# A decoder trunk's up-projection from seven block products in place of eight

## The chip, the cores and the metric

The kernel runs on one core of a Trainium2 chip. The metric is the device time of one execution in microseconds, lower is better. The core's engines are named as the profile names them: PE (TensorE) multiplies matrices and PEld is its loading of weights, DVE, ACT and POOL work elementwise, SP issues transfers; each has its own instruction stream and waits for others by semaphores.

## The reference

One step of a hybrid decoder: a token mixer with two parallel head groups, then a convolutional feed-forward layer (ConvFFN). One prompt of 2048 rows with 16 meta rows ahead, and 8 samples of 4 rows, go through the same weights. Only the ConvFFN concerns this change:

```python
def conv_ffn(h, buf, w_up, cw, cb, w_down):
    u = h @ w_up                           # (rows, 1024) @ (1024, 6144)
    u, new_buf = causal_dwconv(u, buf, cw, cb)   # 3 taps along the rows
    g, v = u[..., :D_FF], u[..., D_FF:]    # 3072 gate and 3072 value columns
    return (jax.nn.gelu(g) * v) @ w_down, new_buf
```

All is float32.

## The kernel before

**Exactness.** A product of float32 operands is formed from two parts of each operand in a rounded format (`F32R`): `hi` is the operand rounded, `lo` is what is left. `group_mm` and `tile_mm` issue three matmuls for each pair of 128-wide blocks: hi by hi, hi by lo, lo by hi. For weights, `split_w` makes the parts `whi` (ACT, L104) and `wlo` (DVE, L105) each time that a block of 512 KB has been loaded; each of the four super-tiles loads and splits all weights anew. There are two raw slots (`wraw`) and two slots for each part.

**Phases.** `phase_a` runs the mixer in six super-tiles; it ends at 930.4 us of the span. `phase_b` runs the ConvFFN in four super-tiles of 512 prompt rows (`PLAN_B`); the first has 34 rows more (`"m"`: 32 sample rows and 2 meta rows). Phase A's last part writes the normalized, transposed and split rows of the first one (`Normed.turn`, tiles `hhi` and `hlo`).

**One super-tile.** `up_g` and `up_v` run over kk = 0 to 23. Each takes one 128-column group of the up-projection, contracts it in 8 chunks of 128, and so issues 24 matmuls of 512 rows (the first super-tile: 48, in pieces of 274 and 272 rows). ACT copies the product from PSUM to `u`; ACT (L842) and DVE (L844, twice) form the convolution; ACT the gelu (L850); DVE the product `p` and its parts `phi` and `plo`. After each 4 kk (`NB`), `down` multiplies that block's `p` by two loaded blocks of `w_down` for one half of the output columns: for each of four row tiles 12 matmuls of 512 columns, added to `acc` by DVE (L887). In the first super-tile `samples` (L910) also multiplies the raw, unsplit `w_down` block by the sample rows. The first half of a block's downs stands two kk after the block, and the second half after the next block.

**Order.** PE follows the order of the program list (`prog`). DVE, ACT and POOL follow an order that a scheduler made ahead of the run, from `START2` to near the end. Loads are issued on SP in the order in which the weights are used, two ahead (`AHEAD`). All engines are strictly in order.

The reader needs of the code: `load_w`, `split_w` and `group_mm` for the weights, `up`, `up_g`, `up_v` and `down` for the stage, and the loop at the end of `phase_b` for the order.

Of the kernel before, what the change touches and what calls it, by code (L numbers as in the profile page):

```python
# [7 lines left out]
F32 = mybir.dt.float32  # L8
# [8 lines left out]
P = 128  # L17
# [10 lines left out]
PLAN_B = [["m", 0, 1, 2, 3], [4, 5, 6, 7], [8, 9, 10, 11], [12, 13, 14, 15]]  # L28
# [3 lines left out]
NFMAX = 546  # L32
# [3 lines left out]
GT_BUFS = 2  # L36

# side tasks of a super-tile, by the main unit that they follow
# [33 lines left out]
def build(tc, i, o):  # L72
# [5 lines left out]
    with contextlib.ExitStack() as es:  # L78
# [6 lines left out]
        phase = es.enter_context(contextlib.ExitStack())  # L85

# [9 lines left out]
        def load_w(src):  # L96
            raw = wp.tile([P, 1024], F32, name="wraw", tag="wraw", bufs=2)
            ld(raw, src)
            return raw

        def split_w(raw, E=V):
            hi = wp.tile([P, 1024], F32R, name="whi", tag="whi")
            lo = wp.tile([P, 1024], F32R, name="wlo", tag="wlo")
            A.activation(hi, raw, AF.Copy)  # L104
            E.tensor_tensor(lo, raw, hi.bitcast(F32), op=SUB)  # L105
            return hi, lo, raw
# [20 lines left out]
        def rstd_tile():  # L127
            return hp.tile([P, 1], F32, name="rstd", tag="rstd", bufs=8)

        def sum_squares(x, rows, width):  # L130
            ss = hp.tile([P, 1], F32, name="nss", tag="nss", bufs=8)
            junk = hp.tile([P, D], BF16, name="junk", tag="junk", bufs=1)
            A.activation(junk[:rows, :width], x, AF.Square, accum_out=ss[:rows])
            return ss
# [7 lines left out]
        class Normed:  # L142
            """rows of x normalized, transposed and split, tile by tile"""
# [6 lines left out]
            def alloc(self):  # L150
                if self.h is None:
                    self.h = [hp.tile([P, 8, NFMAX], F32R, name=nm, tag=nm) for nm in ("hhi", "hlo")]

            def load(self, q):
                src, off, rows = self.tiles[q]
                x = self.x[q] = hp.tile([P, D], F32, name="x", tag="x", bufs=3)
# [27 lines left out]

        def add(fn, *srcs):
# [16 lines left out]
        h_b = Normed(b_tiles(k, 0, None))  # L202
# [3 lines left out]
        flat = [s for fn, srcs in prog for s in srcs]  # L206
        raws, split, used = [], [], 0
# [3 lines left out]
        for n, (fn, srcs) in enumerate(prog):  # L211
# [5 lines left out]
            ahead = AHEAD if n >= START2 else 0  # L217
            while len(raws) < min(len(flat), used + len(srcs) + AHEAD):
                raws.append(load_w(flat[len(raws)]))
            while len(split) < min(len(flat), used + len(srcs) + ahead):  # L220
                split.append(split_w(raws[len(split)], V if split else G))
            ws = split[used:used + len(srcs)]
# [7 lines left out]
def b_tiles(k, si, acc):  # L230
    tiles, off = [], 0
    for q, t in enumerate(PLAN_B[si]):
        rows = SROWS + 2 if t == "m" else P
        if acc is None:
            tiles.append((lambda t=t: (k.x2m if t == "m" else k.x2d[t], True), off, rows))
        else:
            tiles.append((lambda q=q: (acc[q][1], False), off, rows))
        off += rows
    return tiles
# [38 lines left out]
def phase_a(k, h_b):  # L278
# [27 lines left out]
    def setup():  # L306
        ca = k.phase.enter_context(k.tc.tile_pool(name="ca", bufs=1))
        sp = k.phase.enter_context(k.tc.tile_pool(name="sa", bufs=2))
        E.ca, E.sp = ca, sp
        packed = ca.tile([P, SMALL_W], F32, name="packed", tag="packed")  # L310
# [52 lines left out]
def phase_a_tile(k, E, c, si, columns, norm, norm2, x_src):  # L363
# [9 lines left out]
    def tmp(nm, width=NMAX + 3, bufs=2, rows=P, tag=None):  # L373
        return E.sp.tile([rows, width], F32, name=nm, tag=tag or nm, bufs=bufs)
# [25 lines left out]
    # step sizes  # L400
# [9 lines left out]
    def dt_turn():  # L410
        dt = T_.dt = E.sp.tile([P, 3, 8], F32, name="dt", tag="dt")
# [8 lines left out]
        T_.dtA = E.sp.tile([P, 3, 8], F32, name="dtA", tag="dtA")  # L420
        V.tensor_tensor(T_.dtA[:, :nt, :], dt[:, :nt, :], c["alog"][:, None, :].to_broadcast([P, nt, 8]), op=MUL)
        dh = E.sp.tile([P, 3, 8], F32R, name="dh", tag="dh")
        dl = E.sp.tile([P, 3, 8], F32, name="dl", tag="dl")
# [7 lines left out]
    def decays():  # L431
        """exp of the running, remaining and total sums"""
# [66 lines left out]
    def chunk2(q):  # L499
# [13 lines left out]
        Gm = E.sp.tile([P, 2, P], F32, name="Gm", tag="Gm", bufs=1)  # L513
# [46 lines left out]
    def chunk3(q):  # L560
# [3 lines left out]
        # two heads at a time, each on half of the array's columns  # L564
# [36 lines left out]
    # recurrent unit  # L601
# [109 lines left out]
    # output projection  # L711
# [375 lines left out]
```

## Time and profile before

| | us |
|---|---|
| three runs: lowest, median, highest | 2599.92, 2600.65, 2602.12 |
| span of the profiled execution | 2596.3 |
| PE busy | 2521.5 (97%) |
| DVE, ACT, POOL busy | 1770.5 (68%), 1191.7 (46%), 624.7 (24%) |
| traffic of the transfers | 294.56 MB, mean 113 GB/s |

The profiled execution has no device time of its own on the page beside its span; the span lies 4.4 us under the median of the runs, and that difference is taken for what lies around it. The page gives busy time per engine, groups of instructions with the mean duration of one, and the chain of work that ended last, followed back from the end. A group's row reads: line, engine, operation, output and inputs, shape, count, then busy us and mean ns of one, then the engine's idle time just ahead and what ended it. A row of the chain reads: start in us, duration in us, what ran, how often.

### The profile page before, as it was taken

To read this page: it belongs to the slowest core of one execution; us is meant where nothing else is said; L and a number is where in the kernel's file an instruction comes from. 1 tells how busy PE (TensorE), PEld (TensorE's weight loads), DVE (VectorE), ACT (ScalarE), POOL (GpSimd) and SP (SyncE) were. 2 spreads that over 40 slices of the span, in tenths; PEclk is the share of its full clock that TensorE was granted. 3 is DMA by queue.
4 is the path that set the end of the run, shared out by engine and by line. 5 is a ranking of instruction groups with operands and counts; after the bars stand their busy time and mean duration, and the time that the engine had idled before them with its cause. 6 is when DMAs were issued, how large, how long until landed. Compare 5 with 4: busy or idle time off the path is not lost.

```text
span 2596.3 us, 35012 instructions
## 1 busy us (share of the span) xinstructions
PE 2521.5 (97%) x13242; PEld 2152.7 (83%) x13242; DVE 1770.5 (68%) x2500; ACT 1191.7 (46%) x1861; POOL 624.7 (24%) x945
## 2 busy tenths in 40 slices
PE   7999999999999899999999999999999999999998
PEld 6788888888888799999987888888888888888887
DVE  7878889788888866555557655557655557655555
ACT  5445555455554654334435333335433334433333
POOL 5524333242333322112113111112111111111111
PEclk9999999999999999999999999999999999999999
DMA  5352341523415372222225222224222223222222
GB/s 186 120 178 90 102 168 71 180 90 127 152 66 191 111 237 83 98 82 82 82 82 180 88 92 98 97 98 139 100 94 98 92 95 122 97 91 90 96 98 96
DMA packets 89994, 294.56 MB, mean 113 GB/s; under 512 B 10760, under 2 KB 11144, under 8 KB 89824
## 3 DMA queue, kind: packets, MB, share of 16 engines
q1 hardware_dynamic: 89824, 292.32, 32.8%
q8 instruction: 104, 1.70, 0.3%
q14 instruction: 66, 0.54, 0.1%
HBM read 272.24 MB, written 20.03 MB: 113 GB/s over the span
## 4 chain that ended last, share of the span: by engine, by line
PE 81%; DVE 11%; ACT 3%; DMA 2%; issue 2%; POOL 1%; SPq 0%; DVEq 0%; POOLq 0%; ACTq 0%
PE mm L110 34%; PE yy L110 21%; PE sg L110 21%; DVE cv L397 3%; DVE wlo L105 2%; PE tr L178 1%; ACT whi L104 1%; DVE xi L642 1%; PE yy L567 1%; ACT cv L395 1%; PE sg L617 1%; DMA wraw<-in_w_in 1%; DVE xbc L493 0%; DMA x<-xo 0%; DVE L L520 0%
## 5 line engine op out<-in xcount | busy, mean ns | idle before, releaser
L105 DVE TENSOR_TENSOR wlo<-wraw,whi 128x1024 fp32r<-128x1024 f32 x455 | 565.1, 1243 | 539.8 <-ACT whi L104 538.9
L104 ACT ACTIVATE whi<-wraw 128x1024 fp32r<-128x1024 f32 x456 | 482.8, 1059 | 848.4 <-PE mm L110 425.6
L110 PE MATMUL mm<-hhi,whi 128*128 128x384 f32 (+5 forms) x1920 | 656.8, 342 | 12.8 <-ACT xr L392 9.4
L110 PE MATMUL mm<-hlo,whi 128*128 128x384 f32 (+5 forms) x1920 | 651.3, 339 | 0.9 <-DVE hlo L183 0.9
L110 PE MATMUL mm<-hhi,wlo 128*128 128x384 f32 (+5 forms) x1920 | 651.0, 339 | 0.0
L110 PEld LDWEIGHTS mm<-hhi,whi 128*128 128x128 f32 x1920 | 364.8, 190 | 44.5 <-ACT xr L392 11.2
L110 PEld LDWEIGHTS mm<-hlo,whi 128*128 128x128 f32 x1920 | 364.9, 190 | 28.8 <-DVE hlo L183 1.2
L110 PEld LDWEIGHTS mm<-hhi,wlo 128*128 128x128 f32 x1920 | 364.6, 190 | 24.4
L110 PE MATMUL yy<-hhi,wlo 128*128 128x512 f32 (+1 forms) x960 | 338.7, 353 | 0.0
L110 PE MATMUL yy<-hlo,whi 128*128 128x512 f32 (+1 forms) x960 | 337.7, 352 | 0.0
L110 PE MATMUL yy<-hhi,whi 128*128 128x512 f32 (+1 forms) x960 | 336.8, 351 | 0.0
L839 POOL COPY o_fc<-u 128x2 f32<-128x2 f32 x192 | 139.6, 727 | 767.7 <-ACT u L831 646.3
L844 DVE SCALAR_TENSOR_TENSOR c<-u,fcw,c 128x512 f32<-128x512 f32 (+1 forms) x384 | 293.4, 764 | 33.1 <-ACT c L842 23.4
L110 PE MATMUL sg<-whi,phi 128*128 128x512 f32 x768 | 306.7, 399 | 0.0
L110 PE MATMUL sg<-whi,plo 128*128 128x512 f32 x768 | 301.8, 393 | 0.0
L110 PE MATMUL sg<-wlo,phi 128*128 128x512 f32 x768 | 241.1, 395 | 0.0
L110 PEld LDWEIGHTS yy<-hlo,whi 128*128 128x128 f32 x960 | 180.8, 188 | 26.0
L110 PEld LDWEIGHTS yy<-hhi,whi 128*128 128x128 f32 x960 | 180.9, 188 | 25.4
L110 PEld LDWEIGHTS yy<-hhi,wlo 128*128 128x128 f32 x960 | 180.5, 188 | 24.5
L887 DVE TENSOR_TENSOR acc<-acc,sg 128x512 f32<-128x512 f32 x192 | 130.9, 682 | 76.9 <-PE sg L110 76.9
L110 PEld LDWEIGHTS sg<-whi,phi 128*128 128x128 f32 x768 | 144.5, 188 | 42.3 <-issue 8.4
L110 PEld LDWEIGHTS sg<-wlo,phi 128*128 128x128 f32 x768 | 144.4, 188 | 34.2
(223 smaller groups left out, 3226.3 us busy)
## 6 DMA issues: line engine op xcount, KB each, us to landing
wraw<-in_w_up SPq DMA_DIRECT2D x192, 512.0 KB, 3.5
wraw<-in_w_in SPq DMA_DIRECT2D x120, 512.0 KB, 3.5
wraw<-in_w_down SPq DMA_DIRECT2D x96, 512.0 KB, 3.5
wraw<-in_w_out SPq DMA_DIRECT2D x48, 512.0 KB, 3.5
x<-in_x_p SPq DMA_DIRECT2D x16, 512.0 KB, 5.4
xo<-in_x_p SPq DMA_DIRECT2D x32, 256.0 KB, 4.1
x<-xo SPq DMA_DIRECT2D x32, 256.0 KB, 4.0
acc<-x SPq DMA_DIRECT2D x16, 512.0 KB, 4.8
```

The lines of the kernel that those rows point to most:

```text
L104: A.activation(hi, raw, AF.Copy)
L105: E.tensor_tensor(lo, raw, hi.bitcast(F32), op=SUB)
L110: PE.matmul(ps, l, r, start=(k == 0), stop=(k == len(pairs) - 1))
L178: PE.transpose(ps[:, c * rows:(c + 1) * rows], x[:rows, (c0 + c) * P:(c0 + c + 1) * P], ident[:rows, :rows])
L395: A.activation(cv[:, 3:W], buf[:, 3:W], AF.Identity, scale=w[:, 3:4], bias=b)
L397: V.scalar_tensor_tensor(cv[:, 3:W], buf[:, t:t + NC], w[:, t:t + 1], cv[:, 3:W], op0=MUL, op1=ADD)
L567: PE.matmul(psy[z:z + 64, h // 2 * T:(h // 2 + 1) * T], Q.xdt[:T, h * 64:(h + 1) * 64], Q.L3[:, h, :], start=True, stop=True)
L617: PE.matmul(psa[:, :NC], c["wa"][:, j, :], xc[:, 3:W], start=True, stop=True)
L642: V.tensor_tensor_scan(h[:, 3:W], a4[:, j, 3:W], m4[:, j, 3:W], hc[:, j:j + 1], op0=MUL, op1=ADD)
L839: G.tensor_copy(o_fc[:, g, NS, :], u[:, W - 2:W])
L844: V.scalar_tensor_tensor(cv[:, 2:W], u[:, z:z + W - 2], fcw[:, g, z:z + 1], cv[:, 2:W], op0=MUL, op1=ADD)
L887: V.tensor_tensor(xv, xv, ps[:rows, :], op=ADD)
```

## The change

Each super-tile's rows are cut in two halves (256 rows; 274 in the first, with 16 sample rows and 2 meta rows each), the contraction in two halves of 512, and the columns in a gate block and a value block. The 2 by 2 by 2 block product of one kk then has 8 products of 12 matmuls; Strassen's algorithm (in Winograd's form) needs 7, with sums of the blocks as operands:

- On the rows' side, `Halves.turn` makes seven operand tiles `h0` to `h6` (plain blocks B11, B21, B22 and sums T1 to T4), each in two parts, once for a super-tile. They have one buffer each.
- On the weights' side there are the plain gate block (`whl`, two halves), the plain lower value block (`wv`) and four sums (`ws`, z = 0 to 3). In the first super-tile `Sums.split` makes them on POOL (L958 to L961) in place in the raw slots, splits each (ACT L106, DVE L107), and ACT's queue writes the parts to DRAM (`kept`, L964). The other three super-tiles load the parts from there (L951: 4 times 512 KB for each kk) and load of the value block only its lower half.
- The products' sums go through DVE: `s1` (ACT's copy), `s2`, `s3` and `put` (L1012), which adds the last product into `u`.

The code below is the core of the diff. It also lets go of several buffers to make room (phase A's pools, `acc` from 9 to 5 buffers, `xb` for the rows of the next super-tile with 2), forms a super-tile's rows from freshly loaded `x` (before: from `acc`), and loads `gfin` and `gffn` into one tile.

```diff
-PLAN_B = [["m", 0, 1, 2, 3], [4, 5, 6, 7], [8, 9, 10, 11], [12, 13, 14, 15]]
+PLAN_B = [[0, 1, 2, 3], [4, 5, 6, 7], [8, 9, 10, 11], [12, 13, 14, 15]]
+LOADS_B, SPLITS_B = 4, 3
...
+        class Halves:
+            def norm(self, q):
+                rows, load = self.tiles[q]
+                x = self.x[q] = k.hb.tile([P, D], F32, name="xb", tag="xb", bufs=2)
...
+    class Value:
+        def split(self, E=V):
+            hl = E_tile("wv", 512, 1)
+            k.divide(hl[:, 0], hl[:, 1], self.raw[:, 512:1024], E)
...
+    class Sums:
+        def load(self):
+            if not self.t.first:
+                self.out = E_tile("ws", 512, SUMS)
+                ld(self.out.bitcast(F32), kept[self.kk][self.z])
+        def split(self, E=V):
+            if not self.t.first:
+                return
+            g0, g1, v0, v1 = (x.raw[:, y:y + 512] for x in (self.g, self.v) for y in (0, 512))
+            if self.z == 0:
+                G.tensor_tensor(v1, v0, v1, op=ADD)
+                G.tensor_tensor(v0, g0, v0, op=SUB)
+                G.tensor_tensor(g0, v1, g0, op=SUB)
+                G.tensor_tensor(g1, g1, g0, op=SUB)
+            hl = self.out = E_tile("ws", 512, SUMS)
+            k.divide(hl[:, 0], hl[:, 1], (g0, v0, v1, g1)[self.z], E)
+            A.dma_start(kept[self.kk][self.z], hl.bitcast(F32))
...
+    def product(t, wts, z):
+        ps = psum(next(banks))
+        h = t.norm.h[z]
+        k.mms(ps[:, :t.N], [(wts[y1][:, n * P:(n + 1) * P], h[:, y2, n, 0:t.N])
+                            for n in range(4) for y1, y2 in ((0, 0), (0, 1), (1, 0))])
+        return ps
...
+    def second_part(t, kk):
+        def fn(v, w2, w3, w1, w4):
...
+            ps = product(t, (w2[:, 0], w2[:, 1]), T2)
+            q.s2, q.s3 = (tmp(nm, NHALF, 1)[:, :N] for nm in ("s2", "s3"))
+            V.tensor_tensor(q.s2, q.s1[:, :N], ps[:, :N], op=ADD)
+            ps = product(t, (w3[:, 0], w3[:, 1]), T3)
+            V.tensor_tensor(q.s3, q.s2, ps[:, :N], op=ADD)
+            ps = product(t, (w1[:, 0], w1[:, 1]), T1)
+            q.uv = tmp("u", UW, 3)
+            put(t, q.uv, 1, ps, q.s3)
+            V.tensor_tensor(q.s2, q.s2, ps[:, :N], op=ADD)
...
+    def third_part(t, kk):
+        def fn():
+            q = t.prev
+            put(t, q.uv, 0, product(t, (q.v[:, 0], q.v[:, 1]), T4), q.s3)
+            cv = conv(t, 24 + kk, q.uv)
+            put(t, q.ug, 1, product(t, (q.w4[:, 0], q.w4[:, 1]), B22), q.s2)
+            cg = conv(t, kk, q.ug)
...
+        for kk in range(24):
+            g = k.Plain(i["w_up"][kk])
+            v = Value(t, kk, g)
+            s2 = [Sums(t, kk, z, g, v) for z in range(4)]
+            add(first_part(t, kk), g)
+            if kk:
+                add(third_part(t, kk - 1))
...
+            add(second_part(t, kk), v, *s2)
```

One half of a block's downs now stands between the third and the second part at kk = 5, 6, 9, 10, 13, 14, 17, 18 and 21; the other three stand behind kk = 23.

The first place is PE in the first super-tile. Before, the rows of one group follow those of the group ahead of it; here is the end of a gate group's second piece and the start of the value group:

```order
L110 MATMUL mm_9438<-hhi_9121,whi_9325 128x272
L110 MATMUL mm_9438<-hlo_9122,whi_9325 128x272
L110 MATMUL mm_9438<-hhi_9121,wlo_9326 128x272
L110 MATMUL yy_9479<-hhi_9121,whi_9329 128x274
L110 MATMUL yy_9479<-hlo_9122,whi_9329 128x274
L110 MATMUL yy_9479<-hhi_9121,wlo_9330 128x274
```

Now, for kk = 7 (sums 10568 to 10713) with what stands around it; `h5`, `h6`, `h4` are T2, T3, T1, `h0`, `h1` are B11, B21, `h3` is T4 and `h2` is B22:

```order
L126 MATMUL yy_10623<-h0_8973,whl_10558 128x274 x12
L126 MATMUL mm_10638<-h1_8974,whl_10558 128x274 x12
L126 MATMUL tr_10654<-h3_8976,wv_10387 128x274 x12
L126 MATMUL yy_10676<-h2_8975,ws_10554 128x274 x12
L126 MATMUL mm_10731<-h5_8978,ws_10568 128x274 x12
L126 MATMUL tr_10747<-h6_8979,ws_10619 128x274 x12
L126 MATMUL yy_10761<-h4_8977,ws_10709 128x274 x12
L126 MATMUL mm_10782<-h0_8973,whl_10717 128x274 x12
```

Two groups of 48 matmuls have become seven of 12; the two products of kk = 6 that use `wv` and the last sum stand behind the first two of kk = 7.

The second place is POOL in the same stretch. Before it only copies the rows that the convolution carries over:

```order
L824 COPY u_10398<-st_fc_9386 128x8x2
L839 COPY o_fc_9392<-u_10115 128x2
L838 COPY o_fc_9392<-u_10183 128x16
L824 COPY u_10470<-st_fc_9386 128x8x2
L839 COPY o_fc_9392<-u_10183 128x2
L824 COPY u_10538<-st_fc_9386 128x8x2
```

Now the four sums of kk = 7 stand between such copies (`wraw2` is the raw value block, `wraw` the raw gate block):

```order
L1078 COPY o_fc_9388<-u_10615 128x2
L1075 COPY o_fc_9388<-u_10615 128x16
L958 TENSOR_TENSOR wraw2_10548<-wraw2_10548 128x512
L959 TENSOR_TENSOR wraw2_10548<-wraw_10546,wraw2_10548 128x512
L960 TENSOR_TENSOR wraw_10546<-wraw2_10548,wraw_10546 128x512
L1078 COPY o_fc_9388<-u_10418 128x2
L961 TENSOR_TENSOR wraw_10546<-wraw_10546 128x512
```

POOL's work on one kk has grown by four operations on 128 by 512 elements, in a row, each on what the one ahead wrote.

The third place is ACT there. Before, for one group and a half:

```order
L104 ACTIVATE whi_9896<-wraw_9894 128x1024
L836 ACTIVATE u_9832<-mm_9861 128x272
L842 ACTIVATE c_9889<-u_9832,fcb_9384,fcw_9382 128x560
L833 ACTIVATE u_9900<-yy_9902 128x8x4
L834 ACTIVATE u_9900<-yy_9902 128x242
```

Now, for kk = 7 (`wk7_0` is a sum's place in DRAM, L1057 the gelu):

```order
L1024 ACTIVATE s1_10636<-yy_10623 128x274
L106 ACTIVATE wv_10561<-wraw2_10548 128x512
L1080 ACTIVATE c_10672<-u_10615,fcb_9384,fcw_9382 128x560
L106 ACTIVATE ws_10568<-wraw_10546 128x512
L106 ACTIVATE ws_10619<-wraw2_10548 128x512
L1080 ACTIVATE c_10694<-u_10418,fcb_9384,fcw_9382 128x560
L964 DMA wk7_0_123<-ws_10568 128x1024
L964 DMA wk7_1_124<-ws_10619 128x1024
L1057 ACTIVATE c_10694<-c_10694 128x560
L106 ACTIVATE ws_10709<-wraw2_10548 128x512
L106 ACTIVATE ws_10713<-wraw_10546 128x512
```

Before, the splits stood among the copies out of PSUM; now one split of the value block and four splits of sums do, the last two of them behind the gelu, and ACT issues the writes.

The fourth place is SP's loads around a down call of the first super-tile. Before:

```order
L98 DMA wraw_10324<-in_w_up 128x1024
L98 DMA wraw_10392<-in_w_up 128x1024
L98 DMA wraw_10464<-in_w_down 128x1024
L98 DMA wraw_10532<-in_w_down 128x1024
L98 DMA wraw_10604<-in_w_up 128x1024
```

Now, around kk = 5 (L929 loads a value block):

```order
L929 DMA wraw2_10089<-in_w_up 128x1024
L117 DMA wraw_10083<-in_w_up 128x1024
L929 DMA wraw2_10321<-in_w_up 128x1024
L117 DMA wraw_10085<-in_w_down 128x1024
L117 DMA wraw_10087<-in_w_down 128x1024
L117 DMA wraw_10315<-in_w_up 128x1024
```

The value blocks have two slots of their own; gate blocks and `w_down` blocks still share two, and a gate block's slot is now also the place of two of the sums.

More of the change, by code (lines that the diff above doesn't have):

```diff
@@ L127, in rstd_tile, with sum_squares @@
         def rstd_tile():
[L128 to L133, printed above, removed]
+            return hp.tile([P, 1], F32, name="rstd", tag="rstd", bufs=4)
+        def sum_squares(x, rows, width, ss=None):
+            if ss is None:
+                ss = hp.tile([P, 1], F32, name="nss", tag="nss", bufs=4)
+            A.activation(junks[-1]()[:rows, :width], x, AF.Square, accum_out=ss[:rows])
             return ss
@@ L216, in build @@
                 begin.close()
[L217 to L222, printed above, removed]
+            b = n > k.begin_b
+            bound = len(flat) if b else next(z for z, w in enumerate(flat) if hasattr(w, "late"))
+            while loaded < min(bound, used + len(srcs) + (LOADS_B if b else AHEAD)):
+                flat[loaded].load()
+                loaded += 1
+            while split < min(bound, used + len(srcs) + (SPLITS_B if b else AHEAD if n >= START2 else 0)):
+                flat[split].split(*(() if split else (G,)))
+                split += 1
+            ws = [z.out for z in flat[used:used + len(srcs)]]
             used += len(srcs)
@@ L227, in build, with b_halves, samples, rows @@
             fn(*ws)
[L230 to L239, printed above, removed]
+def b_halves(k, si):
+    tiles, pairs = [], []
+    if si == 0:
+        def samples(x):
+            k.G.memset(x[:64], 0.0)
+            for r, a, n in ((0, 0, 16), (16, SROWS, 2), (32, 16, 16), (48, SROWS, 2)):
+                k.ld(x[r:r + n], k.x2m[a:a + n])
+            return x
+        tiles.append((50, samples))
+        pairs.append(((0, 0), (0, 32), MA, 0))
+    base, off = len(tiles), MA if si == 0 else 0
+    for z, q in enumerate((0, 2, 1, 3)):
+        def rows(x, q=q):
+            k.ld(x, k.x2d[PLAN_B[si][q]])
+            return x
+        tiles.append((P, rows))
+        if z % 2:
+            pairs.append(((base + z - 1, 0), (base + z, 0), P, off + z // 2 * P))
+    return k.Halves(tiles, pairs)
 def softplus_small(k, pool, x, n):
@@ L803, in phase_b @@
         t.si, t.first = si, si == 0
-        t.rows = [SROWS + 2 if z == "m" else P for z in PLAN_B[si]]
-        t.N = sum(t.rows)
-        t.W = F0 + 2 + (t.N - SROWS - 2) if t.first else t.N + 2
-        t.NP = t.N - SROWS - 2 if t.first else t.N
-        t.acc = []
-        t.norm = h_b if t.first else k.Normed(b_tiles(k, si, t.acc))
-        t.p, t.ss = {}, {}
+        t.N = NHALF if t.first else 256
+        t.u0 = F0 if t.first else 0
+        t.W = t.u0 + 2 + 512
+        t.acc, t.p, t.pm, t.ss = {}, {}, {}, {}
@@ new lines, in halves, with put @@
+    def halves(w, y):
+        return [w[z][:, y * 512:(y + 1) * 512] for z in range(2)]
+    B11, B21, B22, T4, T1, T2, T3 = range(7)
+    def put(t, u, half, ps, s):
+        N = t.N
+        parts = [(u[:, 2 + 256 * half:258 + 256 * half], 0, 256)]
+        if t.first:
+            u6 = u[:, 0:F0].rearrange("p (b k) -> p b k", k=6)[:, 4 * half:4 * half + 4, 2:6]
+            a = F0 + (2 + 256 if half else 0)
+            parts = [(u[:, a:F0 + 258 + 256 * half], 18 if half else 16, N), (u6, 0, 16)]
+        for out, a, b in parts:
+            src, oth = ps[:, a:b], s[:, a:b]
+            if b == 16:
+                src, oth = s4(src), s4(oth)
+            V.tensor_tensor(out, oth, src, op=ADD)
@@ L913, in samples @@
             if half == 0:
-                t.sacc = tmp("sacc", D, 1)
+                t.sacc = tmp("acc", D, 5)
             V.tensor_copy(t.sacc[:, hs], ps)
```

383 lines of the change are left out of this document (237 added, 146 removed), and 6 rows, old and new, of the table SLOTS.

## The prediction

> **What bounds the kernel now.** I read the stages first, then the chain that ended last within a stage, then the groups for the price of one instruction. The stages are phase A and the four super-tiles of phase B; the columns are length, then busy time of PE, PEld, DVE, ACT and POOL, granted clock, DMA share, GB/s:
>
> ```profile
> 0.00:930.40 930.40, 863.14 (x4971) 764.70 (x4972) 773.19 (x1238) 511.48 (x880) 348.61 (x438) 0.99 0.39 133
> 930.40:1378.80 448.40, 448.25 (x3025) 407.69 (x3025) 262.92 (x347) 186.05 (x323) 85.91 (x167) 1.00 0.30 103
> 1378.80:1783.70 404.90, 404.90 (x1761) 327.73 (x1761) 247.79 (x309) 167.87 (x226) 66.87 (x117) 1.00 0.31 106
> 1783.70:2188.05 404.35, 404.35 (x1762) 328.05 (x1761) 246.85 (x308) 167.38 (x225) 63.20 (x117) 1.00 0.30 103
> 2188.05:2596.30 408.25, 400.88 (x1729) 324.55 (x1727) 239.74 (x300) 158.96 (x209) 60.08 (x108) 0.99 0.28 98
> ```
>
> In phase B PE never waits: it is busy for 448.25 of 448.40 us, 404.90 of 404.90. So fewer matmul columns are worth their full time there, as long as PE still doesn't wait; and any wait that the change brings into phase B is paid in full, since there is no idle time of PE to hide it in. The chain of waits shows what one unit of work costs PE (start, duration, what, how often), first super-tile first, a full-width one last:
>
> ```profile
> 939.24 6.09 PE yy L110 x48
> 945.33 6.07 PE mm L110 x48
> ...
> 1116.10 1.00 PE sg L910 x8
> 1117.10 11.39 PE sg L110 x48
> ...
> 1378.80 5.58 PE mm L110 x24
> ...
> 1445.55 11.20 PE sg L110 x48
> ```
>
> A matmul of 272 or 274 rows takes 6.08/48 = 0.127 us, one of 512 takes 5.58/24 = 0.2325. A kk in the first super-tile (gate and value group) costs 12.15 us, and one with half a block's downs behind it 12.15 + 12.4 = 24.6.
>
> **The gain on PE.** Two groups per kk become seven products of 12. At the pace of before the first super-tile would fall by 24 × 12 × 0.127 = 36.6 us. For the others I need the pace of 256 rows, which phase A's last tile shows:
>
> ```profile
> 863.17 2.82 PE mm L110 x24
> ```
>
> That is 0.1175 us; I take 0.120, because every 12 matmuls now change both operand tiles. A super-tile of 256-row products is 24 × 84 × 0.120 = 241.9 us, its 576 down matmuls 576 × 0.2325 = 133.9. The turn of the next tile's rows is eight groups of four transposes, 0.44 us each by the row below, 4 us.
>
> ```profile
> 1372.77 0.44 PE tr L178 x4
> ```
>
> Ahead of the turn stand, for each row tile, a load and the norm (groups, and the last row from the table of loads, us from issue to landing):
>
> ```profile
> L133 ACT ACTIVATE junk<-x 128x1024 bf16<-128x1024 f32 x20 | 21.1, 1054 | 13.0 <-DMA x<-in_x_p 6.6 <-DMA x<-x 6.3
> L138 POOL TENSOR_SCALAR rstd<-nss 128x1 f32<-128x1 f32 x32 | 13.6, 425 | 172.7 <-ACT junk L133 169.4 <-ACT u L833 2.1 <-ACT xr L387 0.7
> L139 POOL TENSOR_TENSOR rstd<-rstd,neghalf 128x1 f32<-128x1 f32 x32 | 21.9, 685 | 2.5
> L168 DVE SCALAR_TENSOR_TENSOR x<-x,rstd,gain 128x1024 f32<-128x1024 f32 x20 | 25.7, 1284 | 16.1 <-POOL rstd L139 15.9
> ...
> acc<-x SPq DMA_DIRECT2D x16, 512.0 KB, 4.8
> ```
>
> Here is a new wait: `xb` has two buffers, so the third and fourth row tile are loaded only after the first two have been turned: load 4.8, sum of squares 1.05, `rstd` 0.43 + 0.69, scaling 1.28, together 8.3, with one row tile's downs of 12 × 0.2325 = 2.8 over it: about 6 us of idle PE per transition, 0 if the scheduler finds other cover, 8 without any. Super-tiles 2 and 3 then come to 241.9 + 133.9 + 4 + 6 = 386; the last has no turn but the 7.4 us of idle time that it has now (408.25 − 400.88), 383. Together −18.9 − 18.4 − 25.2 = −62.5. The same wait at the end of phase A, where the rows of the first super-tile pass through `xb`, I put at +8 (0 to 10).
>
> The other work of these three tiles is covered by PE: no weight of the up-projection but the plain gate and half a value block is split any more, and DVE's sum operations are new. Per kk DVE has two gate-and-value convolutions, product parts, splits and seven short sums, by the rows of the next fence at most 4 × 0.80 + 0.69 + 0.69 + 1.24 + 0.69 + 7 × 0.41 = 9.4 us under PE's 10.1. Tight, but the sums' loads lie ahead by four.
>
> **The loss: a loop in the first super-tile.** There the sums are made, and the waits go round in a circle with PE on it. `wv` has one buffer. So: T4 of kk−1 reads `wv` → ACT may write the next `wv` → DVE its second part → POOL L958 may overwrite that raw half → L959 → L960 → ACT and DVE split z = 0 → T2 of kk. PE has between T4 and T2 only B22, 12 matmuls or 1.5 us. The prices:
>
> ```profile
> L522 POOL TENSOR_TENSOR xdd<-xdt,ex 128x512 f32<-128x512 f32 x16 | 21.5, 1342 | 33.9 <-DVE xdt L517 33.9
> L585 POOL TENSOR_TENSOR S<-S,ex 128x512 f32<-128x512 f32 x16 | 19.7, 1229 | 25.4 <-PE yy L579 19.9 <-ACT gq L660 3.1 <-DVE xi L623 2.4
> L661 POOL TENSOR_TENSOR sacc<-sacc,gq 128x384 f32<-128x384 f32 x24 | 30.2, 1259 | 70.1 <-ACT gq L660 70.1
> L105 DVE TENSOR_TENSOR wlo<-wraw,whi 128x1024 fp32r<-128x1024 f32 x455 | 565.1, 1243 | 539.8 <-ACT whi L104 538.9
> L104 ACT ACTIVATE whi<-wraw 128x1024 fp32r<-128x1024 f32 x456 | 482.8, 1059 | 848.4 <-PE mm L110 425.6 <-PE sg L110 272.1 <-PE yy L110 69.7
> L183 DVE TENSOR_TENSOR hlo<-tr,hhi 128x512 fp32r<-128x512 f32 x64 | 43.4, 685 | 7.1 <-ACT hhi L182 6.9
> L182 ACT ACTIVATE hhi<-tr 128x512 fp32r<-128x512 f32 x64 | 37.6, 595 | 66.1 <-PE tr L178 66.0
> L514 DVE TENSOR_TENSOR Gm<-tr,packed 128x256 f32<-128x256 f32 x16 | 6.6, 413 | 0.5 <-PE tr L512 0.5
> L844 DVE SCALAR_TENSOR_TENSOR c<-u,fcw,c 128x560 f32<-128x560 f32 x96 | 76.9, 801 | 4.6 <-DMA sel<-in_sel 2.8
> L850 ACT ACTIVATE c<-c 128x560 f32<-128x560 f32 x24 | 16.2, 673 | 15.2 <-DVE c L844 15.0
> L870 DVE TENSOR_TENSOR p<-c 128x512 f32<-128x512 f32 x72 | 49.8, 692 | 2.5
> L867 DVE TENSOR_TENSOR pm<-c 128x32 f32<-128x32 f32 x24 | 4.6, 192 | 0.8
> ```
>
> Three POOL operations of 512 are 3 × 1.29 = 3.9 us (mean of the first two rows; the third row, 1.26 us for 384 elements, would make it 5.0). The first chain, from T4's end: `put` on DVE 0.6 (413 ns and a small one); in two of three cases a whole weight block's second part stands ahead on DVE, 1.24, so 0.8; `wv` second part 0.69; POOL 3.9; split 0.60 + 0.69: 7.3 us. A second chain starts at T2's end: `s2` 0.41, the last convolution step 0.80, gelu 0.67, behind which ACT's order puts the split of z = 2, then on DVE `pm` 0.19, `p` 0.69, second part 0.69: 3.4 us until T1 can run on, with T3 over part of it. On the loop stand T2, T1, B11, B21 and T4, 60 matmuls less 4 that need only a first part, 56 × 0.127 = 7.1. One kk: 7.1 + 7.3 + 3.4 = 17.8, against 12.15 now.
>
> That leaves PE idle for some 6 us once and 2 us once in each kk, and the clock answers to that. Windows at the end of phase A (PE alone: busy, clock, DMA share, GB/s):
>
> ```profile
> 846.00:850.00 4.00, 4.00 (x24) 0.68 0.36 131
> 851.00:854.50 3.50, 0.48 (x5) 0.97 0.41 150
> 854.50:858.00 3.50, 3.46 (x17) 0.55 0.42 150
> 858.00:862.00 4.00, 4.00 (x36) 1.00 0.00 0
> ```
>
> After 3 us with little on PE the clock was 0.55 for the next 3.5 us, then full. Half a clock for 3.5 us is at most 1.7 us of lost work; not each stall meets it, and part of it falls into the next wait, so +0.9 per kk: 18.7 (16 with POOL at 1.0 and no clock loss, 21 with POOL at 1.7). [...]
>
> In a kk with downs the loop is longer. The second `w_down` block takes the raw slot of the first, so it is loaded only behind the sample matmuls on that one, and ACT's order splits it behind all four sums of that kk, so behind POOL's fourth operation. The load (B22 1.5, samples 0.5, landing 4.8 by the row of `acc`) is the shorter way; the other gives from T4's end 0.6 + 1.24 + 0.69 + 4 × 1.29 + ACT 0.60 + 1.06 + DVE 1.24 and the handing over (0.2 to 0.3 us at each of seven semaphores) = 12.1 us, until the first row tile's third chunk can run. Then 41 of the 48 down matmuls are left, 41 × 0.2325 = 9.5, and the up products T2, T3, T1, B11, B21, T4, 72 × 0.127 = 9.1: 30.7, with 1.2 for clock 32 (27.5 if the second block is early, 35 with slow POOL), against 24.6.
>
> First super-tile: start 5, 15 × 18.7 = 280.5, 9 × 32 = 288, the rest (three down calls 33.5, last products, turn, samples, idle time between them) 59: 632, against 448.4: +184. Its bounds by the same terms: 15 × 16 + 9 × 27.5 + 55 = 542 (+94) and 15 × 21 + 9 × 35 + 70 = 700 (+252).
>
> The writes of the sums (50 MB, ACT's queue) and DVE's and ACT's added work in this tile cost nothing more: DVE has about 13 us in 18.7. If the loop were shorter, DVE would be late next.
>
> **Sum.** 2596.3 + 8 + 184 − 62.5 = 2725.8 us of span; the median lies 4.4 over the profiled span, so 2730.
>
> **Rivals.**
>
> *The loop is hidden and the kernel gets faster.* For it speaks that PE's work itself falls (by 36.6 in the first super-tile, 62.5 behind it) and that POOL is idle for 80% of this stage, so its operations could be shorter than phase A's busy ones. If POOL's operations took half (0.65), no block stood ahead on DVE and the second chain lay under T3, a kk would cost 7.1 + 4.6 + 1 = 12.5 and a kk with downs 25: first super-tile 187 + 225 + 59 = 471, and the end 2596.3 + 8 + 23 − 62.5 + 4.4 = 2569. It decides where a kk of the first super-tile loses less than (62.5 − 8)/24 = 2.3 us on the mean, that is at 14.4 us without downs; the wait from T4 to T2 would have to be under 4 us. Against it: no row shows POOL under 1.2 us for 512 elements. 7%.
>
> *The downs stay covered.* The second `w_down` block is split in time, so that only the kk without downs lose: 26 instead of 32, −54: 2676. 15%.
>
> *The transfers bound super-tiles 2 to 4.* A kk there loads 2.88 MB (four sums, one gate block, half a value block), against 1.05 now.
>
> ```profile
> 1378.80:1384.30 5.50, 5.50 (x25) 4.43 (x25) 4.50 (x7) 4.70 (x9) 3.00 (x5) 1.00 0.91 247
> 1384.30:1400.90 16.60, 16.60 (x73) 13.44 (x72) 14.93 (x17) 8.65 (x12) 7.42 (x10) 1.00 0.77 272
> ```
>
> At full share these give 247/0.91 = 271 and 272/0.77 = 353 GB/s, so 10.6 or 8.2 us for 2.88 MB against PE's 10.1. At 271, with the down blocks' loads between, 15 kk of three tiles lose 0.5 to 1.6 us: +24 to +72, 2754 to 2802. Against it: a whole tile moves 84 MB in 386 us, 218 GB/s. 18%.
>
> **Chances.** The forecast (both loops, transfers hidden) 57%, around 2730 with 2690 to 2775; downs covered 15%, transfers 18%, faster 7%, and 3% for an end within 0.2% (5 us, which is about what the measurement can tell). The range reaches from 2640, under the second case, to 2810 over the third. Slower 0.90, same 0.03, faster 0.07.
>
> **What would show it.** In the first super-tile PE busy some 70%, with T2's matmuls waiting for DVE's second part of z = 0 and that for L960; POOL L958 to L961 at 1.2 to 1.4 us; the granted clock under 1.0 there alone. Super-tiles 2 to 4 near 386, 386 and 383 us with PE over 97% busy, and idle PE of about 6 us at each transition, ended by transposes that wait for `xb`. The prediction is wrong if T4 to T2 takes under 4 us in the first tile, or if PE waits for loads of `ws` in the later ones.

## The result, and the profile after

The changed kernel takes 2871.26 us (median; 2869.09 to 2875.07) against 2601.1 for the kernel before beside it: a ratio of 1.1043, 95% interval 1.1027 to 1.1058. The forecast was slower, at 2730 with a range from 2640 to 2810: the direction was right, but the time lies over the range, and the loss of 270 us is twice the 130 of the forecast.

I cut both spans at the last transpose of each turn, which both kernels have. Before, the pieces are 930.1, 442.8, 407.8, 404.3 and 411.3 us. After (length, busy time of PE, PEld, DVE, ACT, POOL, granted clock, DMA share, GB/s):

```profile
0.00:974.70 974.70, 880.34 (x4977) 779.28 (x4978) 777.65 (x1249) 512.56 (x892) 326.82 (x447) 0.96 0.41 128
974.70:1674.10 699.40, 492.54 (x2679) 415.73 (x2677) 398.77 (x677) 209.89 (x321) 206.03 (x257) 0.83 0.38 138
1674.10:2077.30 403.20, 387.14 (x2651) 355.28 (x2649) 285.72 (x467) 161.10 (x238) 44.41 (x126) 0.99 0.64 227
2077.30:2472.90 395.60, 381.20 (x2626) 352.69 (x2625) 280.71 (x461) 159.42 (x232) 45.11 (x122) 0.99 0.64 226
2472.90:2867.20 394.30, 383.23 (x2631) 353.91 (x2629) 274.72 (x456) 150.49 (x219) 40.35 (x118) 0.99 0.60 213
```

So phase A lost 44.6 us, the first super-tile 256.6, and the other three gained 4.6, 8.7 and 17.0: +270.9, the difference of the spans. In the first super-tile PE is busy 70% of the time at a clock of 0.83. The chain of waits over one kk without downs there shows the loop (start, duration, what, how often):

```profile
1287.24 2.65 PE tr L126 x10
...
1293.65 1.54 PE mm L126 x10
...
1303.70 1.76 POOL wraw L958
...
1305.53 1.65 POOL wraw L959
...
1307.25 1.27 POOL wraw L960
...
1308.54 0.64 ACT ws L106
...
1309.20 1.22 DVE ws L107
...
1310.47 2.65 PE yy L126 x10
```

From T2 of one kk to T2 of the next are 23.2 us. Each of T2 and T1 shows ten of its twelve matmuls; the first two need only a first part and run ahead. T2's ten take 2.65 us, T1's ten 1.54. Windows over T2 and over T1 of one kk show the granted clock (third number from the end):

```profile
1287.24:1289.60 2.36, 2.36 (x10) 2.36 (x11) 1.26 (x2) 0.00 (x0) 0.61 (x2) 0.50 0.67 269
1293.65:1295.20 1.55, 1.55 (x12) 1.55 (x13) 1.15 (x2) 0.01 (x1) 0.00 (x0) 1.00 0.49 114
```

In this kk, behind the long wait (5.4 us up to T2's first two matmuls) the granted clock was 0.50; behind the short one of 1.3 us ahead of T1 it was 1.00.

What the forecast did not have lies ahead of L958; here are lines of PE, ACT, POOL and SP from the timeline of that stretch (start, duration, then in brackets the idle time before and what ended it):

```profile
1294.22 0.33 SPq L117 DMA_DIRECT2D wraw<-in_w_up  x1
1298.07 1.70 PE L126 MATMUL mm<-h,wv 128*128 128x274 f32 x12
1300.70 1.06 ACT L106 ACTIVATE whl<-wraw 128x1024 fp32r<-128x1024 f32 x1 [3.56 <-DMA wraw<-in_w_up]
1301.66 0.61 ACT L106 ACTIVATE wv<-wraw 128x512 fp32r<-128x512 f32 x1
1303.70 1.75 POOL L958 TENSOR_TENSOR wraw<-wraw 128x512 f32<-128x512 f32 x1 [3.12 <-DVE wv L107]
```

T4, which frees `wv`, is over at 1299.8; but ACT's order has the split of the next gate block ahead of the split of `wv`, and that waits until 1300.70 for its load. The load was issued only at 1294.22, when DVE had made the last second part out of that raw slot (z = 2 and 3 stand behind the gelu, and were done at 1294.20), and it took 6.5 us. L958 starts 3.9 us after T4, where the forecast's terms ahead of it come to 2.1 (0.6 + 0.8 + 0.69). In the 14 kk without downs counted below this distance is 3.6 to 5.4 us, 4.1 on the mean. Over the stage, the groups of the loop's operations read:

```profile
L959 POOL TENSOR_TENSOR wraw<-wraw,wraw 128x512 f32<-128x512 f32 x24 | 40.1, 1670 | 1.4
L958 POOL TENSOR_TENSOR wraw<-wraw 128x512 f32<-128x512 f32 x24 | 34.3, 1427 | 84.3 <-DVE u L1012 48.9 <-DVE wv L107 35.5
L960 POOL TENSOR_TENSOR wraw<-wraw,wraw 128x512 f32<-128x512 f32 x24 | 33.8, 1407 | 1.4
L961 POOL TENSOR_TENSOR wraw<-wraw 128x512 f32<-128x512 f32 x24 | 30.6, 1273 | 0.5
L107 DVE TENSOR_TENSOR ws<-wraw,ws 128x512 fp32r<-128x512 f32 x96 | 74.5, 814 | 58.1 <-ACT ws L106 58.1
```

L958 to L960 together cost 4.5 us, the forecast had 3.9. At the turn between super-tiles 2 and 3 (waits of PE: total, times, longest), and in the table of loads:

```profile
PE tr L225 <- DVE xb L215: 13.6, 2, 9.0
...
wk<-ws ACTq DMA_DIRECT2D x96, 512.0 KB, 4.7
...
wraw<-in_w_up SPq DMA_DIRECT2D x120, 512.0 KB, 4.9
```

Two waits for the next rows, 13.6 us, stand where the forecast had 6. A 512 KB block of `w_up` now takes 4.9 us from issue to landing at the median (before: 3.5).

For the first super-tile I give below the mean distance of two successive L960 in kk without downs (14 of them) and with downs (9). Here they are 24.3 and 31.7 us, against 18.7 and 32 in the forecast.

### The profile page after: what moved, and what is told of

The parts are those of the page before. It is cut to its first block, busy times and chain, and to the rows that moved or that the text cites. A ratio compares the mean times of both kernels' runs of the same rounds, so it can differ in the third digit from the quotient of the medians.

```text
span 2867.2 us, 42030 instructions
## 1 busy us (share of the span) xinstructions
PE 2524.5 (88%) x15554; PEld 2256.9 (79%) x15554; DVE 2017.6 (70%) x3306; ACT 1193.5 (42%) x1899; POOL 662.7 (23%) x1069
## 4 chain that ended last, share of the span: by engine, by line
PE 64%; DVE 15%; issue 7%; POOL 5%; ACT 4%; DMA 4%; SPq 0%; POOLq 0%; DVEq 0%; ACTq 0%
PE mm L126 23%; PE sg L126 16%; PE tr L126 10%; PE yy L126 10%; DVE whl L107 3%; DVE cv L496 3%; DMA wraw<-in_w_down 2%; POOL wraw L959 1%; ACT whl L106 1%; POOL wraw L960 1%; DVE ws L107 1%; POOL wraw L958 1%; ACT ws L106 1%; DMA xb<-x 1%; DVE c L1082 1%
## 5 line engine op out<-in xcount | busy, mean ns | idle before, releaser
L126 PE MATMUL sg<-whl,ph 128*128 128x512 f32 x2304 | 585.6, 412 | 27.5 <-ACT whl L106 11.7
L107 DVE TENSOR_TENSOR whl<-wraw,whl 128x1024 fp32r<-128x1024 f32 x359 | 452.7, 1262 | 206.1 <-ACT whl L106 205.9
L126 PEld LDWEIGHTS sg<-whl,ph 128*128 128x128 f32 x2304 | 446.9, 197 | 157.3 <-ACT whl L106 16.4
L106 ACT ACTIVATE whl<-wraw 128x1024 fp32r<-128x1024 f32 x360 | 380.1, 1057 | 390.8 <-PE sg L126 105.2
L126 PE MATMUL mm<-hhi,whl 128*128 128x384 f32 (+2 forms) x1920 | 487.8, 334 | 7.3 <-ACT xr L491 4.7
L126 PEld LDWEIGHTS mm<-hhi,whl 128*128 128x128 f32 x1920 | 348.3, 195 | 13.4 <-ACT xr L491 6.3
L1082 DVE SCALAR_TENSOR_TENSOR c<-u,fcw,c 128x512 f32<-128x512 f32 (+1 forms) x384 | 307.1, 828 | 43.1 <-ACT c L1080 41.2
L126 PE MATMUL mm<-hlo,whl 128*128 128x384 f32 (+2 forms) x960 | 316.1, 329 | 0.9 <-DVE hlo L199 0.9
L126 PE MATMUL mm<-h,ws 128*128 128x256 f32 (+1 forms) x1536 | 222.9, 296 | 47.9 <-ACT ws L106 41.3
L126 PE MATMUL yy<-h,ws 128*128 128x256 f32 (+1 forms) x1584 | 226.7, 293 | 41.5 <-ACT ws L106 31.8
L126 PE MATMUL tr<-h,ws 128*128 128x256 f32 (+1 forms) x1488 | 214.6, 295 | 43.5 <-ACT ws L106 37.7
L1057 ACT ACTIVATE c<-c 128x512 f32<-128x512 f32 (+1 forms) x96 | 61.6, 642 | 218.4 <-DVE c L1082 198.8
```

Of the source, the lines that this page charges most:

```text
L126: PE.matmul(ps, l, r, start=(k == 0), stop=(k == len(pairs) - 1))
L1057: A.activation(cg[:, 2:W], cg[:, 2:W], AF.Gelu_apprx_tanh)
L1082: V.scalar_tensor_tensor(cv[:, 2:W], u[:, z:z + W - 2], fcw[:, g, z:z + 1], cv[:, 2:W], op0=MUL, op1=ADD)
```

## The experiments

Each of the first ten is one run with a profile, beside one run of the kernel before on the same chip (2599.97 to 2603.45 us). "First super-tile" is always the stretch between last transposes, 699.4 us in the changed kernel.

**Shorter sums.**

```diff
-                G.tensor_tensor(v1, v0, v1, op=ADD)
+                G.tensor_tensor(v1[:, :8], v0[:, :8], v1[:, :8], op=ADD)
...
```

> The four POOL operations that make the sums run on 8 columns in place of 512 (so the sums are wrong), with the same reads, writes and waits between them; everything else is left. The scheduler, told of shorter operations, also puts the splits of z = 2 and 3 ahead of the gelu on ACT. Theory L (a loop from T4 over wv, POOL and z = 0 to T2 sets the pace of the first super-tile, and POOL's three operations of 1.27 to 1.75 us are over 4 us of it): a kk without downs falls from 24.3 to 16 to 19 us, one with downs from 31.7 to 25 to 28; the first super-tile from 696 to 530 to 590 us, the time to 2700 to 2765. Rival D (the load of the next gate block, 6.5 us from issue to landing, sets it, and POOL only fills the same time): less than 40 us, 2830 or more.

2760.42 us; first super-tile 588.0. A kk without downs falls to 16.6 us, into the loop's range, but not by POOL alone: L958 to L960 take 1.1 us in place of 4.5, and DVE's second part of z = 0 takes 0.68 in place of 1.21, together 3.9 of the 7.7 us. The rest has no run of its own: the new order of the splits on ACT, which the expectation names, came with it, and the granted clock rose from 0.83 to 0.88. A kk with downs stays at 31.1: there my path through POOL's fourth operation isn't the only one of that length. PE's waits over phase B name the other:

```profile
PE sg L1124 <- DMA wraw<-in_w_down: 45.4, 14, 4.9
```

The second `w_down` block is issued only behind the sample matmuls on the first, and its load and split take as long.

**Few writes.**

```diff
-            A.dma_start(kept[self.kk][self.z], hl.bitcast(F32))
+            if self.kk == 0:
+                A.dma_start(kept[self.kk][self.z], hl.bitcast(F32))
...
-                ld(self.out.bitcast(F32), kept[self.kk][self.z])
+                ld(self.out.bitcast(F32), kept[0][self.z])
```

> Only the four sums of kk = 0 are written to DRAM, and super-tiles 2 to 4 load these for every kk (so their results are wrong); loads keep their number and size, 92 of 96 writes of 512 KB and their issue on ACT are gone. Theory L: the writes cost only what they delay the gate block's load (4.9 us in the median against 3.6 without them), about 1 us of a kk: the first super-tile 696 to 665 to 685 us, the time 2840 to 2862. Rival W (the writes and their issue on ACT are the 5.6 us per kk that a kk without downs lies over the forecast): 84 us or more less, 2790 or below.

2809.91 us; first super-tile 636.2, a kk without downs 20.1, with downs 31.0. Between the two expectations, and far from the nothing of the forecast: without the writes, and with the order that the scheduler then makes, the stage is 63 us shorter. The same stretch of its timeline:

```profile
1261.12 0.33 SPq L117 DMA_DIRECT2D wraw<-in_w_up  x1
1267.77 1.70 PE L126 MATMUL mm<-h,wv 128*128 128x274 f32 x12
1266.79 1.05 ACT L106 ACTIVATE whl<-wraw 128x1024 fp32r<-128x1024 f32 x1
1269.55 0.63 ACT L106 ACTIVATE wv<-wraw 128x512 fp32r<-128x512 f32 x1 [1.71 <-issue]
1271.00 1.27 POOL L958 TENSOR_TENSOR wraw<-wraw 128x512 f32<-128x512 f32 x1 [0.62 <-DVE wv L107]
```

The gate block is split before T4 ends (1269.5), `wv` directly behind T4, and L958 starts 1.5 us after it in place of 3.9. That is 2.4 of the 4.2 us per kk. But an order moved as well: with fewer instructions on ACT the scheduler put the splits of z = 2 and 3 ahead of the gelu. T1's own wait (1.3 us in the kk shown of the changed kernel) is gone by it, and the gate block's slot comes free earlier: its load is issued 3.2 us after the start of T2's ten matmuls in place of 7.0, and takes 4.1 us in place of 6.5 (the medians from 978 to 1500 us of the span are 3.7 and 4.9). By the times of these two kk, as an estimate, either change alone would have landed it before T4's end.

The run with shorter sums has all the writes and, in most kk, the same new order. From T4's end to L958 it takes 2.7 us on the mean of the kk without downs, against 4.1 in the changed kernel and 1.7 here, although its loads of `w_up` take 6.1 us at the median. So a part of the 63 us belongs to the order; how much the writes alone cost is open.

**Small writes.**

```diff
+            else:
+                A.dma_start(kept[self.kk][self.z][:, :, :4], hl[:, :, :4].bitcast(F32))
```

> As the run with few writes, but the 92 writes are issued as before on ACT, each of 4 columns of each part (4 KB in place of 512 KB); super-tiles 2 to 4 load the sums of kk = 0 for every kk. Theory B (the writes cost by their traffic, which makes the gate block's load late): like the run with few writes, the first super-tile 630 to 650 us, the time 2800 to 2825. Rival I (they cost by their issue on ACT, 0.33 us and more each, ahead of gelu and splits): the first super-tile 670 us or more, 2845 or more.

2833.21 us; first super-tile 656.3, a kk without downs 20.8, with downs 32.2. It lies between the two expectations: 43 of the 63 us go with the bytes and the new order, which the kk without downs have here too; 20 stay with the issues or with writes of many small pieces. Which, is open.

**A third gate slot.**

```diff
-    CB, SUMS = 3, 6
+    CB, SUMS = 3, 5
...
-            g = k.Plain(i["w_up"][kk])
+            g = (Gate if kk % 3 == 2 else k.Plain)(i["w_up"][kk])   # Gate: raw slot of its own
```

> Every third gate block of the up-projection gets a raw slot of its own (4 KB, from ws: 5 buffers in place of 6), so a gate block's load need not wait until the block two before it has been split to the last sum. Theory L: ACT no longer waits for that load ahead of the split of wv (62 us in 16 waits), 1 to 2 us less in each kk without downs: first super-tile 660 to 685 us, time 2835 to 2860. Rival D (the load sets the pace): a kk without downs falls to about the forecast 18.7, 2790 or below. Against both: with 5 buffers of ws a wait for one could come in, over 2871.

2845.99 us; first super-tile 670.4, which is in the range, but not for the reason: a kk without downs is 23.5 on the mean, hardly less. ACT still waits up to 5.11 us for a gate block ahead of `wv`, since the scheduler pulled a later block's split forward. The gain is in kk with downs: three of the nine fell to 25.2 to 26.5 us, where the second `w_down` block found a free slot.

**Two `wv`.**

```diff
-            hl = E_tile("wv", 512, 1)
+            hl = E_tile("wv", 512, 2)
...
-    CB, SUMS = 3, 6
+    CB, SUMS = 3, 5
```

> The split lower value block wv gets a second buffer (4 KB, from ws: 5 buffers in place of 6), so its split, POOL's sums and the split of z = 0 no longer start behind T4 of the kk before. Theory L: the loop is cut there; a kk without downs falls from 24.3 to 15 to 18 us (what is left is the second chain from T2 to T1), the first super-tile to 540 to 600 us, the time to 2715 to 2775. Rival D (the gate block's load, issued only behind the last sum's split, sets it): at most 2 to 3 us of a kk, 2810 or more.

2710.98 us; first super-tile 539.0, just past the better end of the loop's expectation. One tile of 4 KB per partition is worth 160 us, together with the order that the scheduler can make with it, in which the sums start ahead of T4's end in 22 of 23 kk: what was slow is the circle from T4 over `wv` to T2, not the amount of work. PE's longest waits there are now those for `w_down` (34.8 us in 9).

**A third row buffer.**

```diff
-                x = self.x[q] = k.hb.tile([P, D], F32, name="xb", tag="xb", bufs=2)
+                x = self.x[q] = self.room(q)   # q == 3: a slot of wraw2
...
+            if kk == 23 and not last:
+                for z in (0, 1, 3):
+                    add(lambda z=z, n=nxt.norm: n.norm(z))
```

> The rows of the next super-tile get a third buffer in phase B (a slot of the value blocks, idle at that time, so no more memory), the one that is turned first of the second pair; three of the four row tiles are loaded and normed from kk = 23 on, and the fourth behind the third turn in place of the fourth. Theory X (the idle 14 us of PE at each of three transitions are waits for the rows' loads into two buffers): 9 to 11 us less at each, the time 2838 to 2848. Rival Y (the waits come from the order of ACT, POOL and DVE there, or the loads queue behind weight loads anyway): 3 to 4 us less at each, 2858 to 2864.

2833.57 us, 38 less: the three stretches with a turn at their end fall by 11.3, 13.3 and 13.4 us, to 688.1, 389.9 and 382.2. In the stretch where PE waited 13.6 us for `xb`, its longest wait is now 1.2 us, for DVE's additions:

```profile
PE sg L126 <- DVE acc L1107: 1.6, 2, 1.2
```

**The two parts of a plain weight apart.**

```diff
-                hl = wp.tile([P, 2, 1024], F32R, name="whl", tag="whl")
-                divide(hl[:, 0], hl[:, 1], self.raw, E)
+                hi = wp.tile([P, 1024], F32R, name="whi", tag="whi")
+                lo = wp.tile([P, 1024], F32R, name="wlo", tag="wlo")
+                divide(hi, lo, self.raw, E)
```

> The two parts of a plain weight block stand in two tiles again, as before the change, in place of one; the memory is the same. Theory M (phase A is longer by 44 us because the merged tile holds a slot until both parts are read): phase A, 974.7 us to the last turn, falls by 10 to 25 us, and the time to 2846 to 2861. Rival S (the merged tile costs nothing; phase A is longer because the scheduler was given other pools and other work at its end and made another order): phase A changes by under 5 us or in either direction with the order, the time 2865 or more.

2854.68 us; phase A 957.6, that is 17.1 of its 44.6 us back, every other stretch within 2.2 us. (In the six other runs that leave phase A's code as it is, it takes 976.9 to 979.6.) The first 200 us of the three kernels (before, changed, parts apart):

```profile
0.00:200.00 200.00, 177.52 (x1030) 148.98 (x1031) 156.84 (x303) 104.65 (x206) 84.42 (x141) 0.97 0.46 160
```

```profile
0.00:200.00 200.00, 164.93 (x900) 136.62 (x901) 140.52 (x264) 92.95 (x188) 75.48 (x133) 0.90 0.41 137
```

```profile
0.00:200.00 200.00, 176.73 (x1027) 148.10 (x1028) 156.15 (x303) 103.84 (x206) 83.87 (x141) 0.97 0.49 160
```

The changed kernel has done 130 matmuls fewer by then, with parts apart 3 fewer. Whether the merged tile holds its slot longer, or only led the scheduler to another order, this run doesn't tell.

**A plain first super-tile.** If making the sums is not the cost, but waiting for them, the first super-tile can use the eight plain blocks and leave the sums to the later ones.

```diff
+            add((gate_part if t.first else first_part)(t, kk), g)
...
+    def plain(t, w, u, E):
+        for half, zs in enumerate(((B11, B21), (T4, B22))):   # T4's tile holds the fourth plain block
+            ps = psum(next(banks))
+            k.mms(ps[:, :t.N], [(w[y][y1][:, n * P:(n + 1) * P], t.norm.h[z][:, y2, n, 0:t.N])
+                                for y, z in enumerate(zs) for n in range(4) for y1, y2 in ((0, 0), (0, 1), (1, 0))])
...
+DOWNS = (5, 6, 9, 10, 13, 14, 17, 18, 21)   # these gate blocks have a raw slot of their own
```

> The first super-tile forms its products from the eight plain blocks (24 matmuls into one bank, 96 per kk, no sums on its path); POOL still makes the sums and ACT writes them for the other three super-tiles, which use seven products. wv has two buffers, ws four, the gate blocks of kk with downs have a raw slot of their own, and the transitions are as with the third row buffer. Theory L (the first super-tile's 699 us are the loop of the sums, not the cost of making them): it falls to 450 to 485 us, the time to 2595 to 2640. Rival E (ACT, DVE and POOL are full with the sums' splits and writes, so they set the pace even off PE's path): 14 to 16 us per kk, the first super-tile 510 or more, the time 2660 or more.

2652.91 us; first super-tile 509.2, phase A 979.7, then 388.7, 381.0 and 392.5. Between the two: most of the loss is gone, but not all. PE waits 20.9 us for `w_down` loads and 11.3 for a gate block's split.

**Early rows.**

```diff
+                if self.plain and q > 1:   # rows into operand tiles h4 to h6, unused there
+                    z = k.hb.tile([P, 2, 4, NHALF], F32R, name=f"h{q + 2}", tag=f"h{q + 2}")
...
-        20: "rstd0 ssd2 turn2 turn3 norm2", 21: "ssd3 turn4 turn5", 22: "rstd1 turn6", 23: "turn7 norm3",
+        20: "rstd0 ssd2 turn2 turn3 norm3", 21: "ssd3 turn4 turn5 norm4", 22: "rstd1 turn6", 23: "turn7",
```

> As the one with the plain first super-tile, and at the end of phase A three of the five row tiles are loaded into operand tiles that the plain first super-tile leaves free, two steps earlier. Theory X2 (two waits of some 8 to 10 us at the end of phase A are those loads): 15 to 20 us less than that run, 2575 to 2622. Rival S2 (phase A's end is slow by its order of small work, the loads only fill the same time): under 6 us less.

2640.74 us, 12 less; phase A 964.8, 14.9 less. That is short of the 15 to 20 us expected, but over the rival's 6: the wait for rows is a large part of phase A's end.

**Raw slots.**

```diff
+    class Gate(k.Plain):
+        def load(self):   # gate and value block into one of h4 to h6
+            z = 4 + len(taken) % 3
+            taken.append(k.hb.tile([P, 2, 4, NHALF], F32R, name=f"h{z}", tag=f"h{z}"))
```

> As the plain first super-tile with early rows, with three differences: in the first super-tile each gate block and value block is loaded into one of three operand tiles that stand empty there (three raw slots in place of two, and w_down has two of its own), ws has five buffers, and the two parts of a plain weight stand in tiles of their own. Theory R (what is left of the first super-tile over PE's work, 511 us against 448, is a loop of load, sums and slot, with loads of 6 to 8 us): it falls to 450 to 475 us, and phase A by 10 to 17, together a time of 2565 to 2600, level with or under the kernel before. Rival E (POOL, DVE and ACT are full there): 490 us or more, 2600 or more.

2587.76 us; first super-tile 475.7, phase A 946.9: in the range of theory R for the time, and for the first super-tile at its upper end (475). PE's waits for loads are gone there; PE's longest are now for DVE:

```profile
PE sg L127 <- DVE acc L1167: 12.1, 9, 3.0
```

**ACT in place of DVE for the value copies.**

```diff
-            plain(t, [(z[:, 0], z[:, 1]) for z in v], u, V)
+            plain(t, [(z[:, 0], z[:, 1]) for z in v], u, A)
```

> As the plain first super-tile with raw slots (2587.8 us), and the value block's products, too, are copied out of PSUM by ACT in place of DVE. Theory V (what is left in its first super-tile, 476 us against 448, is DVE late with its work: 385 of 450 us busy, and PE waits for DVE's additions to acc): 30 us less of DVE there, the first super-tile 455 to 470 us, the time 2568 to 2583. Rival T (loads at 6 us from issue to landing set it): within 4 us of 2587.8.

A miss: 2608.57 us in five rounds, a ratio to before of 1.0036 (1.0024 to 1.0049), with a first super-tile of 496.9. DVE has less to do, but the copies now stand on ACT, in order, with splits that wait for POOL. ACT's longest wait there:

```profile
ACT ws L106 <- POOL h L991: 86.9, 23, 4.4
```

With the copies on DVE (the next run) this wait is as long, 89.6 us in 22, so it is not new; what is new is that the copies stand in the same order with it. The loss lies in the kk with downs, 24.6 us against 21.7, and PE's longest wait is still for DVE's additions, 20.3 us against 12.0. That the copies' place on ACT is the cause is argued, not shown.

**The better one, timed.** The kernel with raw slots once more, in five rounds.

> The kernel of the plain first super-tile with raw slots once more, timed in five rounds against the kernel before. If its one run of 2587.8 us was no accident: 2583 to 2593 us, a ratio of 0.993 to 0.997. If it was one: level, 0.998 to 1.002.

2586.55 us (2585.41 to 2589.37) against 2600.8: a ratio of 0.9949, 95% interval 0.9935 to 0.9963. It takes 0.5% less than the kernel before, a small gain but outside the interval, and 9.9% less than the changed one: seven products where the sums are loaded, eight where they have to be made. Its stages up to the end of the second super-tile:

```profile
0.00:942.70 942.70, 868.32 (x4977) 768.53 (x4978) 773.96 (x1240) 511.87 (x882) 353.89 (x439) 0.98 0.42 134
942.70:1419.00 476.30, 446.15 (x2967) 403.63 (x2965) 406.06 (x531) 227.72 (x414) 232.15 (x255) 0.99 0.55 199
1419.00:1807.90 388.90, 384.46 (x2652) 353.77 (x2649) 288.08 (x467) 161.78 (x238) 52.28 (x126) 1.00 0.66 235
```

## Why the prediction was right or wrong

The forecast's span was 2725.8 us and the measured one is 2867.2. Of the 141 us between them about 73 lie in the first super-tile, 37 in phase A and 32 in the other three super-tiles.

- *Right: the loop.* T4, `wv`, POOL, z = 0, T2 is the chain in the trace, and cutting it with one more buffer gives 160 us back. In the kk shown 10.7 us lie between T4's end and T2's ten matmuls, so the rival in which the loop is hidden (under 4) fell.
- *Wrong: the loop's first chain, from T4's end to L958, and with it "the writes of the sums … cost nothing more".* The forecast had 2.1 us there, and 4.1 were measured. It counted the gate block's second part on DVE (0.8), but took that block's load as landed. The path has three links more. The block's raw slot is let go only by the last sum's split, which stands behind the gelu. With the writes the load takes longer. And on ACT the block's first part stands ahead of the split of `wv`. Without the writes, and with the order that comes with that, the distance is 1.7 us and the first super-tile takes 636.2 us against the forecast's 632. In the term: a kk without downs was 18.7 in the forecast, 24.3 in the run and 20.1 without writes. What the writes and the order cost each is open.
- *Mis-sized: POOL's three operations*, 3.9 us in the forecast, 4.5 in the run, and the second part of z = 0, the one on the loop, 1.21 in place of 0.69. The higher end for POOL (5.0) had been named.
- *Right in number, incomplete in its path: a kk with downs*, 31.7 us against 32. With POOL's work taken away it stays at 31.1, since the second `w_down` block's load, which I called the shorter way, is as long. No run shows the 0.2 to 0.3 us that the sum has for each handing over; the steps of the chain above follow each other within 0.02 to 0.07 us. That the total came out is partly luck.
- *Wrong: phase A*, +44.6 against +8 (0 to 10), where the forecast counted nothing but the wait for rows. Of this, 17 us hang on the merged tile of a weight's two parts, which it did not look at, and 15 on the wait for rows (measured in the kernel with a plain first super-tile). With both undone phase A is at 942.7 to 946.9; what the last 13 to 17 us are is open.
- *Mis-sized: the transition*, 6 us in the forecast, 13.6 in the trace, and 38 us in all for three of them. I let one of the two waits count, and the load of rows on the path takes 7.0 us at the second turn (the row below) and 6.3 at the third, not 4.8.

```profile
2054.73 7.00 DMA xb<-x
```

- *Right: PE bounds the steady part of super-tiles 2 to 4*, and transfers stay hidden:

```profile
1790.00:1890.00 100.00, 100.00 (x705) 93.38 (x704) 70.48 (x119) 38.93 (x53) 7.34 (x27) 1.00 0.62 224
```

- *The clock: right that it drops, too small in size.* It is 0.83 over the first super-tile and 0.99 behind it; that phase A falls to 0.96 as well the forecast did not say. T2's ten matmuls take 2.65 us at a clock of 0.50, where T1's take 1.54 at 1.00, and the twelve of T3 behind T2 take 2.12 and 2.42 us in two kk, where twelve at full clock take 1.69. That is 1.5 to 1.8 us in such a kk, against 0.9 in the forecast.

## What to carry to other kernels

A chain of waits that comes back to its start is a loop, and its period is the sum of all links, however idle each engine is; one more buffer at the right link can be worth more than any operation made faster. In such a sum, ask of every instruction ahead of a link on the same in-order engine when its own input lands (here ACT stood 3.56 us before a gate block's load, with the split of `wv` behind it): when its buffer is let go and the load can be issued, and how long the load takes beside new traffic, even on another queue (here 4.9 us at the median with the writes on ACT's queue, 3.7 in the run without them). An experiment that changes what a scheduler sees also changes its order, so compare the orders before a difference is put down to the edit. Where a cheaper product needs operands that have to be made first, use it where they come ready-made, and keep the plain one where they are being made.

## What the runs showed of the hardware

The same POOL operation on 128 by 512 elements takes from 1.26 to 1.76 us (L958 in the changed kernel):

```profile
L958 POOL TENSOR_TENSOR wraw<-wraw x24: 1259/1267/1756, 986.0 to 1610.5; 128x512 f32<-128x512 f32 x24
```

L958 takes 1.75 us in the 8 kk where it starts during one of DVE's convolution steps (L1082). In the 9 where L958 starts first, by 0.03 to 0.06 us, that step takes 1.80 to 1.83 us in place of 0.80; and in the 6 where it starts beside L1012, which reads one input from PSUM, L958 stays at 1.26 to 1.27. DVE's second part of a sum takes 0.68 us at the median; that of z = 0, which runs beside L961, takes 1.2 in all 24 kk, and at most 0.69 where L961 has 8 columns (the run with shorter sums). On this loop the longer durations cost about 1.2 us per kk, an estimate from 4.50 us for L958 to L960 against three times 1.26, and 1.21 against 0.68.

Loads of 512 KB of `w_up`, from 978 to 1500 us of the span, took 3.7 us from issue to landing at the median without the writes of the sums, 4.9 with them and 6.1 in the run with shorter sums, while packets took 21.8%, 38.3% and 47.1% of the 16 DMA engines' time in that stretch.
